# A two-layer diffusion backbone: modulation rows of the second layer made during the first layer's attention instead of beside its experts

## The chip, the core and the metric

The kernel runs on one core of a Trainium2 chip. The core has TensorE (PE in the profile), VectorE (DVE), ScalarE (ACT), GpSimd (POOL) and the DMA queues, of which the kernel uses SyncE's (SP) for nearly all loads and POOL's for gathers, scatters and some tables. The metric is the device time of one execution in microseconds (us), the median of several runs.

## What is computed

Two layers over 1024 latent tokens and 256 context tokens of width 1024. Cut to what matters here:

```python
for l in range(DEPTH):                       # 2 layers
    mod   = silu_c  @ w_ada[l] + b_ada[l]    # 6 x 1024 numbers for the latent tokens
    mod_c = silu_cc @ w_ada[l] + b_ada[l]    # the same for the context tokens
    sh1, sc1, g1, sh2, sc2, g2 = split(mod, 6)
    h = modulate(rms_norm(x, norm1_g[l]), sh1, sc1)
    y, yc = mixer_sublayer(h, hc, ...)       # Fourier | global attention | windowed attention + sink, gated merge
    x = x + g1 * y
    h = modulate(rms_norm(x, norm2_g[l]), sh2, sc2)
    x = x + g2 * expert_choice_ffn(h, ...)   # 16 experts, each takes 128 latent (and 32 context) tokens
    # the same for the context tokens, in layer 0 alone
return rms_norm(x, final_g)
```

`mod` is one row by a 1024 x 6144 matrix. Layer 1 has no context output, so of its modulation the context row is needed for the first 2048 columns alone (shift and scale of the first norm); columns 2048 to 6143 are needed for the latent row only.

## The kernel before

**Stages.** Each layer runs through: norm and modulation, the input projection, attention, the gated merge in chunks of tokens (two of 512 latent tokens, in layer 0 a third of the 256 context tokens), routing (softmax and top-k), and 16 experts. In layer 0 `moe_both` (L1505) runs latent and context tokens of an expert together. Matrix products are made of three passes over pairs (hi, lo): each weight is loaded as float32, ACT casts the hi part (L238), DVE subtracts to get the lo part (L245), and PE multiplies hi by hi, hi by lo and lo by hi. For the first four weight loads of `moe_both` POOL subtracts instead (L243).

**Modulation rows.** They are cut into blocks of 512 columns, called units: `units1` holds layer 1's twelve, the first four with two rows (n = 2), the other eight with one row (n = 1). A unit doesn't use PE for its 1024-deep sum. It multiplies pieces of `w_ada` (128 x 512) by the activation of c, one number a partition, adds eight of them up, and lets PE sum the 128 partitions: two matmuls by a column of ones, for the hi and the lo part of the sum (L337, L338). `ada` (L311) is a generator; `ada_row` (L376) adds the bias row, which it loads from DRAM (L382), multiplies by a norm gain where there is one (L386, L391), and stores the row in DRAM (L399). In the merge of layer 0 the generator runs with ACT doing the products (L351) and POOL the sums (L356): chunk 0 makes layer 0's remaining rows, chunk 1 makes `units1[:6]`. The last six units run in `moe_both`, two steps of the generator at each of the four column blocks of an expert from the second expert on, with POOL doing product and sum, one piece of 256 KB a step: 48 pieces, whose loads (L327) stand in SP's queue among the experts' weight loads (L232).

**Attention.** `attend` records its operations through `Pin`, so all of them have L797 in the profile and keep the order in which they are written on their engine. SP's operations, and those of `ada_row`, aren't pinned: a scheduler puts them where it finds room. 30 groups of queries in layer 0 give 210 steps, one of 128 keys each. A step makes scores on PE into one of two banks (accT), ACT takes the exponential, and PE multiplies by V three steps later (accO). The softmax's maximum comes from a first pass for a later group, spread over the steps: PE makes scores into one of three banks (accS), DVE reduces each to one column of `m` (`rmax`), `mdiag` folds the columns of `m` (and the sink) into `mrs`, and `mrow` transposes that on PE through the same three banks. Where a bank comes up again, `sbank` first runs the reader that was left for it. `outp` copies a group's result out (ACT), for groups with a sink adds the sink's share (DVE), and issues three DMAs on SP; five steps later `recip` takes the reciprocal on DVE of a row that has been to DRAM and back. POOL loads the Fourier tables and is otherwise idle there.

Of the kernel before, what the change touches and what calls it, by code (L numbers as in the profile page):

```python
# [10 lines left out]
F32 = mybir.dt.float32  # L11
F32R = mybir.dt.float32r
# [4 lines left out]
OP = mybir.AluOpType  # L17
AX = mybir.AxisListType
# [90 lines left out]
def f(ap):  # L109
    return ap.bitcast(F32)  # L110
# [7 lines left out]
def hybrid_kernel(ctx, tc, x, c, ctxt, c_ctx, w_ada, b_ada, norm1_g, w_in, q_norm_g, k_norm_g,  # L118
# [17 lines left out]
    def t512(p, n, dt=F32):  # L136
        return tmp.tile([p, n], dt, name="t512")
# [46 lines left out]
    ident = misc.tile([128, 128], F32, name="ident")  # L184
# [11 lines left out]

    gqk = misc.tile([128, 2, 64], F32, name="gqk")
    sinkb = misc.tile([128, 4], F32, name="sinkb")
    mrs = misc.tile([128, 6, 4], F32R, name="mrs")
    mod1 = misc.tile([128, 2, 8, 2], F32, name="mod1")  # L200
    c2 = misc.tile([128, 8, 2], F32, name="c2")
    e2 = misc.tile([128, 4], F32R, name="e2")
# [9 lines left out]
    class Ring:  # L212
# [3 lines left out]
        def load(self, src, kk, n, pool=0):  # L216

            hi, lo, split = self.begin(src, kk, n, pool)
            for _ in split:
                pass  # L220
            return hi, lo
# [605 lines left out]
    def attend(need_ctx, V, S, G, PE):  # L827
# [53 lines left out]
        def prep(g):  # L881
            lab('prep', g['i'])

            for h in range(4):
                PE.transpose(X[0][0:64, 128 * h:128 * h + 128], g["q"][:, 64 * h:64 * h + 64], ident)
            qs = ring("qs", 512, F32R)
            qm = ring("qm", 512, F32R)
            g["qs"], g["qm"] = qs, qm
            g["m"] = st.tile([128, 4, 3], F32, name="m", bufs=4)
            g["us"] = units(g)  # L890
            g["nu"] = len(g["us"]) // 4

        def prep2(g):
            lab('prep', g['i'])
# [35 lines left out]
        def mdiag(g):  # L930
            lab('mdiag', g['i'])
            m = g["m"]
            for i in range(1, g["nu"]):
                V.tensor_max(m[:, :, 0], m[:, :, 0], m[:, :, i])
            if g["sink"]:
                V.tensor_max(m[:, :, 0], m[:, :, 0], sink8)
            g["mr"] = mrs[:, g["i"] % 6]
            V.tensor_copy(g["mr"], m[:, :, 0])

        def mrow(g):  # L940
            lab('mrow', g['i'])
            b = sbank()
            for h in range(4):
                PE.transpose(b[0:1, 128 * h:128 * h + 128], f(g["mr"])[:, h:h + 1], ident)
            S.copy(g["qm"][64:65], b[0:1])

        def scores(g, t):
# [101 lines left out]
        def front():  # L1049
# [25 lines left out]
            mrow(g0)  # L1075
            yield

        def main(hooks):

            ST.extend(acc("T") for _ in range(2))  # L1080
            OB.extend(acc("O") for _ in range(2))
            for o in RINGS["qm"][1:3]:
                qmfill(o)
            fill = fourier_lat(V, S, G, PE, sbank)
            next(fill)
            bk1 = build_k(1, V, S, G, PE, lambda split: X[0])
            kind1 = max(g["s1"] for g in gs if g["ty"] == 1)
            assert min(g["s0"] for g in gs if g["ty"] == 1) >= 20
            for n in range(len(steps) + 4):
                if n < len(steps):  # L1090
                    scores(*steps[n])
                for x in first[n] + acts[n]:
                    x()
                if 2 <= n <= 8:
                    next(bk1, None)
                if n == 9:
                    qmfill(RINGS["qm"][3])
                if n > 8 and n % 2 == 1:
                    next(fill, None)
                if n == kind1 + 6:  # L1100
                    hooks["stage"](G)
                if n == max(kind1 + 12, len(steps) - 30):
                    for _ in fill:
                        pass
                    ld = hooks["weights"](V, S)
                    next(ld)
                if n >= len(steps) - 22 and n % 2 == 0:
                    next(ld, None)
                if 3 <= n < len(steps) + 3:
                    pv(*steps[n - 3])  # L1110
            for _ in ld:
                pass
            return [x for a in acts[len(steps) + 4:] for x in a]
# [391 lines left out]
    def moe_both(l):  # L1505
# [8 lines left out]
        CXL = regr(b + 6144, 1024).rearrange("p (k n) -> p k n", k=8)  # L1514
        X = [regr(b + 7168 + 2560 * i, 2560).rearrange("p (k n) -> p k n", k=8) for i in range(2)]
        ST = [regr(b + 12288, 2560).rearrange("p (k n) -> p k n", k=8)] * 2
        ada_o = [b + 14848 + 512 * i for i in range(5)]
        fill = ada(units1[6:], 1, ada_o[0:2], ada_o[2:3], ada_o[3:5],
                   Pin(V), Pin(G))
        yb = [reg(b + 17408 + 1024 * i, 1024) for i in range(2)]  # L1520
        yc = [reg(b + 19456 + 512 * i, 512) for i in range(2)]
        ycb = reg(b + 20480, 1024)
# [1 line left out]
        for e in range(NE):  # L1524
# [24 lines left out]
            V.tensor_copy(xg[:, :, 288:320], f(CXL[:, :, cc]))  # L1549
            sT = ST[i2]  # L1550
            for fb in range(4):
                for _ in range(2 if e else 0):
                    next(fill, None)
                fs = slice(256 * fb, 256 * fb + 256)
                un = [w_.load(kview(w[l, e, :, fs]), 8, 256, 2 if e == 0 and 2 * fb + t < 4 else 0)
                      for t, w in enumerate((w_gate_e, w_up_e))]
# [43 lines left out]
                V.scalar_tensor_tensor(ycb[0:32, dd], t[0:32], afc[:, e:e + 1], cg2b[0:32, dd], op0=OP.mult, op1=OP.mult)  # L1600
            scatter_add(xd, yb[i2], idxl[:, e:e + 1])
            scatter_add(xcd, ycb[0:32], idx32[:, e:e + 1])
        for _ in fill:
            pass

    def spill(ci, hh, hl, toff, n):
        SP.dma_start(hTd[ci][0], f(hh[toff // 512][:, :, :n]))
# [21 lines left out]
    for l in range(2):  # L1629
# [66 lines left out]
        cut_main()  # L1696
        fills = [iter(())] * 3
        if l == 0:
            todo = [(0, b, 2) for b in (4, 5, 8, 9, 6, 7, 10, 11)] + units1[:6]
            fills = [ada(u, 2, [O_XS + 1024 * i for i in range(2)], [O_XS + 1024 * i for i in range(2, 4)],  # L1700
                         [O_GB + 512 * i for i in range(4)], act=True)
                     for u in (todo[:8], todo[8:], [])]
# [81 lines left out]
```

## Time and profile before

| what | us |
|---|---|
| runs shown (3) | 4038.36, 4061.48, 4057.38; median 4057.38 |
| the profiled execution, its own time | 4049.72 |
| its span, first to last instruction | 4047.9 |
| PE busy in the span | 3726.5 (92%) |
| DVE, ACT, POOL busy | 2803.0, 2023.6, 646.7 |
| attention of layer 0 after the projection | about 262 to 660 |
| merge of layer 0, chunk 1 | about 960 to 1150 |
| experts of layer 0 | about 1400 to 2325 |

How to read it: the span is cut by place, since each stage has its own limit. A window's row gives its length, then for each engine the busy time in it and in brackets the number of instructions (PE, PE's weight loads, DVE, ACT, POOL), the granted TensorE clock as a share of full speed, the mean busy share of the DMA engines, and GB/s. A row of grouped instructions gives line, engine, operation, tiles (output <- inputs), shapes and count, then busy us and the mean ns of one, then the idle time of the engine just before them and what ended it. A timeline row gives start and length in us, then the instruction, and in brackets the idle time before it and what ended that. A row of waits gives who waited for what: us in total, times, longest.

### The profile page before, as it was taken

How to read it: one execution, taken by the hardware profiler on the slowest of the kernel's cores; microseconds unless marked ns; L12 is line 12 of the kernel's file. 1: busy time of each engine (PE TensorE's matmuls, PEld its weight loads, DVE VectorE, ACT ScalarE, POOL GpSimd, SP SyncE). 2: the span in 40 equal slices, each digit the busy share in tenths (PEclk: the TensorE clock that was granted, in tenths of full speed). 3: DMA queues.
4: the chain of work that ended last, by engine and by line, in shares of the span. 5: the costliest groups of instructions: out<-in, count | busy, mean ns of one | idle time of the engine just before them, and what ended most of it. 6: DMA issues, size and time to landing. Idle time of an engine off the chain costs nothing.

```text
span 4047.9 us, 52394 instructions
## 1 busy us (share of the span) xinstructions
PE 3726.5 (92%) x19185; PEld 2952.5 (73%) x19185; DVE 2803.0 (69%) x5007; ACT 2023.6 (50%) x3181; POOL 646.7 (16%) x598
## 2 busy tenths in 40 slices
PE   7989998899999698999999979999999994999997
PEld 4766655688789687788888867666588884777775
DVE  5855556957658677888777667455445746899988
ACT  4235555534424365556666542555433331777775
POOL 0230003512400423342000013100000002011100
PEclk9999999999999799999999989999999996999999
DMA  7332013555556477777877550401235435999996
GB/s 249 128 57 65 12 53 105 179 170 186 188 174 204 164 251 255 235 258 253 263 251 246 189 192 19 96 14 52 74 99 177 148 118 177 351 376 376 380 376 243
DMA packets 491503, 749.07 MB, mean 185 GB/s; under 512 B 27216, under 2 KB 291664, under 8 KB 489962
## 3 DMA queue, kind: packets, MB, share of 16 engines
q1 hardware_dynamic: 453996, 654.14, 46.9%
q0 software_dynamic: 32064, 72.70, 7.2%
q10 hardware_dynamic: 5184, 18.88, 1.2%
q8 instruction: 151, 2.47, 0.3%
q14 instruction: 108, 0.88, 0.1%
HBM read 675.21 MB, written 70.52 MB: 184 GB/s over the span
## 4 chain that ended last, share of the span: by engine, by line
PE 58%; DVE 15%; issue 14%; DMA 7%; ACT 4%; POOL 2%; SPq 0%; POOLq 0%; DVEq 0%; ACTq 0%
PE accA L259 10%; PE accA L261 10%; PE accA L260 10%; PE accO L797 8%; PE accT L797 5%; DVE a_r L245 4%; PE accS L797 4%; PE accA L1566 2%; PE accA L1564 2%; DMA a_f<-in_w_in_dram 2%; DMA a_f<-in_w_ada_dram 1%; ACT a_r L238 1%; DMA a_f<-in_w_down_e_dram 1%; DVE a_f L358 1%; POOL a_f L797 1%
## 5 line engine op out<-in xcount | busy, mean ns | idle before, releaser
L245 DVE TENSOR_TENSOR a_r<-a_f,a_r 128x1024 fp32r<-128x1024 f32 (+1 forms) x1008 | 1220.2, 1230 | 370.3 <-ACT a_r L238 346.1
L238 ACT CAST a_r<-a_f 128x1024 fp32r<-128x1024 f32 (+1 forms) x1024 | 1030.6, 1029 | 700.2 <-DVE a_r L245 281.5
L259 PE MATMUL accA<-a_r,a_r 128*128 128x512 f32 (+1 forms) x2816 | 1039.7, 370 | 33.3 <-DVE a_f L1596 8.7
L261 PE MATMUL accA<-a_r,a_r 128*128 128x512 f32 (+1 forms) x2816 | 1028.4, 367 | 21.7 <-DVE a_r L245 15.3
L260 PE MATMUL accA<-a_r,a_r 128*128 128x512 f32 (+1 forms) x2816 | 1032.3, 367 | 10.5 <-DVE a_f L1169 6.2
L259 PEld LDWEIGHTS accA<-a_r,a_r 128*128 128x128 f32 x2816 | 539.6, 192 | 152.5 <-DVE a_f L1596 11.5
L261 PEld LDWEIGHTS accA<-a_r,a_r 128*128 128x128 f32 x2816 | 538.8, 192 | 116.2 <-DVE a_r L245 19.8
L260 PEld LDWEIGHTS accA<-a_r,a_r 128*128 128x128 f32 x2816 | 539.8, 192 | 96.9 <-DVE a_r L245 8.5
L1566 PE MATMUL accA<-a_r,a_r 128*128 128x320 f32 x2048 | 537.9, 314 | 16.3 <-DVE a_f L1574 15.4
L1564 PE MATMUL accA<-a_r,a_r 128*128 128x256 f32 x1792 | 485.1, 283 | 0.0
L797 DVE TENSOR_REDUCE m<-accS 128x1 f32<-128x512 f32 (+2 forms) x536 | 284.8, 559 | 199.4 <-PE accS L797 195.5
L797 PE MATMUL accO<-a_f,a_f 128*65 128x512 f32 (+1 forms) x976 | 418.6, 525 | 0.0
L797 ACT ACTIVATE a_f<-accT 128x512 f32<-128x512 f32 x408 | 243.4, 597 | 312.7 <-PE accT L797 308.7
L1566 PEld LDWEIGHTS accA<-a_r,a_r 128*128 128x128 f32 x2048 | 373.6, 190 | 20.4 <-DVE a_f L1574 17.5
L1564 PEld LDWEIGHTS accA<-a_r,a_r 128*128 128x128 f32 x1792 | 345.7, 193 | 0.6
L797 PE MATMUL accT<-a_r 128*128 128x512 f32 x512 | 257.2, 583 | 1.6 <-ACT a_f L797 1.6
L259 PE MATMUL accO<-a_r,a_r 128*128 128x512 f32 (+1 forms) x464 | 186.8, 405 | 19.2 <-ACT a_f L561 11.5
L797 PEld LDWEIGHTS accT<-a_r 128*128 128x128 f32 x512 | 97.4, 191 | 125.7 <-issue 107.5
L260 PE MATMUL accO<-a_r,a_r 128*128 128x512 f32 (+1 forms) x464 | 182.7, 396 | 2.8 <-DVE a_r L245 2.6
L261 PE MATMUL accO<-a_r,a_r 128*128 128x512 f32 (+1 forms) x464 | 181.5, 394 | 0.2 <-DVE a_r L472 0.2
L797 PEld LDWEIGHTS accO<-a_f,a_f 128*65 128x65 f32 x976 | 128.7, 138 | 44.5 <-issue 3.3
L356 POOL TENSOR_TENSOR a_f<-a_f,a_f 128x512 f32<-128x512 f32 x84 | 141.5, 1685 | 88.3 <-ACT a_f L351 78.1
(288 smaller groups left out, 4722.6 us busy)
## 6 DMA issues: line engine op xcount, KB each, us to landing
a_f<-in_w_gate_e_dram SPq DMA_DIRECT2D x128, 1024.0 KB
a_f<-in_w_up_e_dram SPq DMA_DIRECT2D x128, 1024.0 KB
a_f<-in_w_down_e_dram SPq DMA_DIRECT2D x128, 1024.0 KB
a_f<-in_w_in_dram SPq DMA_DIRECT2D x60, 1024.0 KB
a_f<-in_w_ada_dram SPq DMA_DIRECT2D x60, 512.0 KB
a_f<-in_w_out_dram SPq DMA_DIRECT2D x20, 1024.0 KB
a_f<-in_w_in_dram SPq DMA_DIRECT2D x36, 512.0 KB
hTd<-a_r SPq DMA_DIRECT2D x8, 2048.0 KB
```

The lines of the kernel that those rows point to most:

```text
L238: S.copy(hi[:, c], raw[:, c])
L245: V.tensor_sub(lo[:, c], raw[:, c], f(hi[:, c]))
L259: PE.matmul(ps, lhsT=lh, rhs=rh, start=start, stop=False)
L260: PE.matmul(ps, lhsT=lh, rhs=rl, start=False, stop=False)
L261: PE.matmul(ps, lhsT=ll, rhs=rh, start=False, stop=stop)
L356: G.tensor_tensor(acc_[0], prod[:, 0] if h == 0 else acc_[0], prod[:, k], op=OP.add)
L358: V.scalar_tensor_tensor(acc_[1], w[:, k], c2[:, kk * h + k, 1:2], zero.to_broadcast([128, 512]) if h + k == 0 else acc_[1], op0=OP.mult, ...
L797: return lambda *a, **k: tc.keep_in_program_order(fn(*a, **k))
L1564: PE.matmul(ps[:, 512 * t:512 * t + 256], lhsT=wl[:, k, fc], rhs=xg[:, k, 0:256], start=False, stop=False)
L1566: PE.matmul(ps[:, 512 * t:512 * t + 320], lhsT=wh[:, k, fc], rhs=xg[:, k, 0:320], start=k == 0, stop=k == 7)
```

## The change

1. `units1[4:]`, all eight units with one row, are made in the main part of layer 0's attention by two new functions. `rows1` does the products and sums on POOL, one piece of 256 KB a call, called at steps 12, 15, 17, 20, 22 and so on (two in five) into two raw buffers and two sums; the cast and the subtraction that split a finished sum go to ACT and DVE three pieces later. `sums_out` then takes one of the three accS banks for the two matmuls, and leaves `ada_row` as that bank's reader.
2. The generator in `moe_both` is gone, and chunk 1 of the merge makes `units1[:4]` instead of `units1[:6]`.
3. `mdiag` makes the maximum in one TENSOR_REDUCE over the columns of `m`; the sink's values are copied into a column of `m` in `prep`. `mrs` becomes plain float32.

```diff
-    mrs = misc.tile([128, 6, 4], F32R, name="mrs")
+    mrs = misc.tile([128, 6, 4], F32, name="mrs")
...
             g["nu"] = len(g["us"]) // 4
+            if g["sink"]:
+                V.tensor_copy(g["m"][:, :, g["nu"]], sink8)
...
             m = g["m"]
-            for i in range(1, g["nu"]):
-                V.tensor_max(m[:, :, 0], m[:, :, 0], m[:, :, i])
-            if g["sink"]:
-                V.tensor_max(m[:, :, 0], m[:, :, 0], sink8)
             g["mr"] = mrs[:, g["i"] % 6]
-            V.tensor_copy(g["mr"], m[:, :, 0])
+            V.tensor_reduce(g["mr"], m[:, :, 0:g["nu"] + g["sink"]], axis=AX.X, op=OP.max)
...
+        def rows1(units, raws, prod, accs):
+            pieces = [(l, b, h) for l, b, _ in units for h in range(8)]
+            def load(i):
+                if i < len(pieces):
+                    l, b, h = pieces[i]
+                    SP.dma_start(reg(raws[i % 2], 512), w_ada[l, 128 * h:128 * h + 128, 512 * b:512 * b + 512])
...
+            for i, (l, b, h) in enumerate(pieces):
+                a = reg(accs[i // 8 % 2], 512)
+                p = reg(prod, 512) if h else a
+                G.tensor_tensor(p, reg(raws[i % 2], 512), c2[:, h, 0:1].to_broadcast([128, 512]), op=OP.mult)
+                load(i + 2)
+                if h:
+                    G.tensor_tensor(a, a, p, op=OP.add)
+                yield
+                if h == 2 and todo:
+                    todo()
+                if h == 7:
+                    def todo(l=l, b=b, a=a):
+                        hi, lo = t512(128, 512, F32R), t512(128, 512, F32R)
+                        S.copy(hi, a)
+                        V.tensor_sub(lo, a, f(hi))
+                        sums.append((l, b, hi, lo))
...
+        def sums_out(l, b, hi, lo):
+            ps = sbank(lambda: ada_row(l, b, ps[0:1], t512(1, 512), n=1))
+            PE.matmul(ps[0:1], lhsT=e2[:, 0:1], rhs=hi, start=True, stop=False)
+            PE.matmul(ps[0:1], lhsT=e2[:, 0:1], rhs=lo, start=False, stop=True)
...
+                if n == 12:
+                    ada1 = rows1(units1[4:] if need_ctx else [], [10752, 11264], 11776, [O_K, O_K + 512])
+                if n >= 12:
+                    if sums and n % 2 == 0:
+                        sums_out(*sums.pop(0))
+                    if n % 5 in (0, 2):
+                        next(ada1, None)
...
-        fill = ada(units1[6:], 1, ada_o[0:2], ada_o[2:3], ada_o[3:5],
-                   Pin(V), Pin(G))
...
-                for _ in range(2 if e else 0):
-                    next(fill, None)
...
-            todo = [(0, b, 2) for b in (4, 5, 8, 9, 6, 7, 10, 11)] + units1[:6]
+            todo = [(0, b, 2) for b in (4, 5, 8, 9, 6, 7, 10, 11)] + units1[:4]
```

How instructions move, at three places. On **POOL**, at the start of layer 0's experts (`hd,idxl` and `hcd,idxc` are the gathers of an expert's latent and context tokens, the second waited for by the first expert; `xd` and `xcd` are its scatters; 128x256 is a weight's lo part, 128x512 the generator's products and sums). Before:

```order
L243 TENSOR_TENSOR a_2048_r<-a_2048_f,a_2048_r 128x256 x2
L797 TENSOR_TENSOR a_512_f<-a_512_f,c_95 128x512
L243 TENSOR_TENSOR a_2048_r<-a_2048_f,a_2048_r 128x256
L797 TENSOR_TENSOR a_512_f<-a_512_f 128x512
L243 TENSOR_TENSOR a_2048_r<-a_2048_f,a_2048_r 128x256
L797 TENSOR_TENSOR a_512_f<-a_512_f,c_95 128x512
L797 TENSOR_TENSOR a_512_f<-a_512_f 128x512
L797 DMA a_1024_f<-hcd,idxc 128x1024
L1406 DMA a_1024_f<-hd,idxl 128x1024
L1410 DMA xd<-a_1024_f,idxl 1024x1024
L1410 DMA xcd<-a_1024_f,idx_131 256x1024
L797 TENSOR_TENSOR a_512_f<-a_512_f,c_95 128x512 x2
```

And now (L1456 and L1460 are the old L1406 and L1410):

```order
L243 TENSOR_TENSOR a_2048_r<-a_2048_f,a_2048_r 128x256 x14
L1456 DMA a_1024_f<-hd,idxl 128x1024
L243 TENSOR_TENSOR a_2048_r<-a_2048_f,a_2048_r 128x256 x6
L797 DMA a_1024_f<-hcd,idxc 128x1024
L1456 DMA a_1024_f<-hd,idxl 128x1024
L1460 DMA xd<-a_1024_f,idxl 1024x1024
L1460 DMA xcd<-a_1024_f,idx_131 256x1024
L1456 DMA a_1024_f<-hd,idxl 128x1024
```

The products and sums are gone from between the lo parts, from before the context gather, and from between scatters and gathers.

On **SP**, in the attention (`sdd`, `od`, `rd` and `rdd` are the DMAs of `outp` and `recip`, of which `rd` waits until `sdd` has landed). Before:

```order
L997 DMA sdd<-a_512_f 1x512
L998 DMA od<-a_512_f 64x4x128
L1000 DMA rd<-sdd 16x32
L998 DMA odc<-a_512_f 64x4x128
L997 DMA sdd<-a_512_f 1x512
L1000 DMA rd<-sdd 16x32
L1006 DMA rdd<-rd 16x32 x2
```

And now (L995 to L1004 are the old L997 to L1006; L1084 is a load of `rows1`, L382 the bias row, L399 the finished row):

```order
L382 DMA t_3446<-in_b_ada_dram 1x512
L998 DMA rd<-sdd 16x32
L1084 DMA a_512_f<-in_w_ada_dram 128x512 x2
L399 DMA modd_71<-t_3445 1x512
L1084 DMA a_512_f<-in_w_ada_dram 128x512
L1004 DMA rdd<-rd 16x32
L1084 DMA a_512_f<-in_w_ada_dram 128x512 x5
L995 DMA sdd<-a_512_f 1x512
L996 DMA od<-a_512_f 64x4x128
L998 DMA rd<-sdd 16x32
```

Eight loads of a unit now stand close together ahead of a group's output, and the bias row stands ahead of them.

On **DVE**, in the attention near step 40 (each `m<-accS` is a row maximum from a bank). Before:

```order
L797 TENSOR_REDUCE m<-accS 128x1 x4
L797 TENSOR_TENSOR m<-m 128x4
L797 TENSOR_TENSOR m<-m,sink_400 128x4
L797 CAST mrs<-m 128x4
L797 TENSOR_REDUCE m<-accS 128x1 x2
```

And now:

```order
L797 TENSOR_TENSOR t_3130<-a_512_f,t_3129 128x512
L797 TENSOR_REDUCE m<-accS 128x1 x4
L797 TENSOR_REDUCE mrs<-m 128x4
L797 TENSOR_REDUCE m<-accS 128x1
L389 TENSOR_TENSOR t_3185<-accS,t_3186 1x512
L797 TENSOR_REDUCE m<-accS 128x1
```

Three small operations are one; the subtraction of a unit's sum and the bias addition stand in the line with the row maxima.

## Rows read from the trace of the kernel before

**Rows 1.** Windows: layer 0's attention, expert 0, experts 1-8, experts 9-15.
```profile
262.00:660.00 398.00, 381.96 (x1678) 236.92 (x1677) 203.65 (x442) 220.31 (x408) 24.53 (x42) 0.99 0.19 47
...
1400.00:1457.00 57.00, 57.00 (x359) 51.37 (x359) 40.66 (x68) 35.00 (x61) 0.98 (x2) 0.97 0.64 213
1457.00:1942.00 485.00, 451.39 (x2780) 394.18 (x2779) 389.44 (x547) 280.88 (x491) 167.37 (x102) 0.96 0.77 251
1942.00:2321.00 379.00, 374.80 (x2394) 332.71 (x2392) 286.28 (x454) 232.65 (x416) 27.02 (x19) 1.00 0.73 239
```
**Rows 2.** Timeline, POOL: the scatters that end the first, ninth and last expert.
```profile
1456.95 1.62 POOL L1410 DMA_INDIRECT xd<-a_f,idxl  x1 [54.71 <-DVE a_f L1596]
...
1941.93 1.58 POOL L1410 DMA_INDIRECT xd<-a_f,idxl  x1 [53.39 <-DVE a_f L1596]
...
2321.43 1.55 POOL L1410 DMA_INDIRECT xd<-a_f,idxl  x1 [49.50 <-DVE a_f L1596]
```
**Rows 3.** Grouped instructions, DVE, 1500 to 1900: experts with the generator.
```profile
L245 DVE TENSOR_TENSOR a_r<-a_f,a_r 128x1024 fp32r<-128x1024 f32 x153 | 206.3, 1360 | 56.7 <-ACT a_r L238 56.3
L1574 DVE TENSOR_TENSOR a_f<-accA,a_f 128x320 f32<-128x320 f32 x50 | 24.2, 484 | 13.5 <-ACT a_f L1573 13.1
L1577 DVE TENSOR_TENSOR t<-t,a_f 128x160 f32<-128x160 f32 x50 | 23.2, 464 | 4.4 <-ACT t L1576 4.4
```
**Rows 4.** Grouped instructions, DVE, 1900 to 2310: experts without it.
```profile
L245 DVE TENSOR_TENSOR a_r<-a_f,a_r 128x1024 fp32r<-128x1024 f32 x178 | 215.4, 1220 | 67.2 <-ACT a_r L238 67.0
L1574 DVE TENSOR_TENSOR a_f<-accA,a_f 128x320 f32<-128x320 f32 x62 | 30.2, 486 | 10.7 <-ACT a_f L1573 9.9
L1577 DVE TENSOR_TENSOR t<-t,a_f 128x160 f32<-128x160 f32 x62 | 19.8, 320 | 6.5 <-ACT t L1576 6.5
```
**Rows 5.** Waits of SP's queue, 1376 to 1900.
```profile
SPq L327 <- POOL a_f L797: 87.9, 32, 7.8
```
**Rows 6.** Timeline, ACT, 1524 to 1537: a weight that came late.
```profile
1534.56 1.04 ACT L238 CAST a_r<-a_f 128x1024 fp32r<-128x1024 f32 x1 [8.97 <-DMA a_f<-in_w_up_e_dram]
```
**Rows 7.** Timeline, POOL, before the first expert.
```profile
1389.57 1.03 POOL L797 TENSOR_TENSOR a_f<-a_f,c 128x512 f32<-128x512 f32 x1
...
1392.09 0.96 POOL L797 DMA_INDIRECT a_f<-hcd,idxc  x1
```
**Rows 8.** Timeline, DVE, before the first expert: the context gather's indices.
```profile
1386.63 0.64 DVE L797 CAST idxc<-accT 32x4 int32<-32x4 f32 x4
```
**Rows 9.** Timeline, PE, before the first expert: what waits for that gather.
```profile
1396.57 1.94 PE L1543 MATMUL accT<-ident,a_f 128*128 128x128 f32 x8 [10.16 <-DMA a_f<-hcd,idxc]
```
**Rows 10.** Timeline, SP, 1060 to 1102: chunk 1 of the merge.
```profile
1068.10 10.55 SPq L327 DMA_DIRECT2D a_f<-in_w_ada_dram  x3
```
**Rows 11.** One line, L337: a unit's matmul.
```profile
L337 PE MATMUL accC<-t,e x32: 387/392/585, 694.0 to 1899.0; 128*2 128x512 f32 x24, 128*1 128x512 f32 x8
```
**Rows 12.** One line, L382: who waited for bias rows.
```profile
  DVE t L389: 8.9, 3
```
**Rows 13.** Waits of PE, 262 to 660: attention of layer 0.
```profile
PE accS L797 <- DVE m L797: 5.7, 7, 2.3
PE accS L797 <- DVE mrs L797: 3.3, 4, 1.5
```
**Rows 14.** Grouped instructions, DVE, 262 to 660: the folding of the maxima.
```profile
L797 DVE TENSOR_TENSOR m<-m 128x4 f32<-128x4 f32 x38 | 5.9, 155 | 0.7
```
**Rows 15.** Waits of DVE, 262 to 660.
```profile
DVE rd L797 <- DMA rd<-sdd: 10.9, 3, 5.9
```
**Rows 16.** Timeline, DVE, 1360 to 1367: the same operation twice.
```profile
1361.05 4.58 DVE L285 SCALAR_TENSOR_TENSOR rsq<-rsy,ss 128x1 f32<-128x1 f32 x1
...
1365.86 0.22 DVE L285 SCALAR_TENSOR_TENSOR rsq<-rsy,ss 128x1 f32<-128x1 f32 x1
```
**Rows 17.** Timeline, POOL, 1359 to 1367: beside that operation.
```profile
1360.28 3.43 POOL L243 TENSOR_TENSOR a_r<-a_f,a_r 128x256 fp32r<-128x256 f32 x5
1363.68 1.25 POOL L797 TENSOR_TENSOR a_f<-a_f 128x512 f32<-128x512 f32 x1
```

More of the change, by code (lines that the diff above doesn't have):

```diff
@@ L943, in mrow @@
             for h in range(4):
-                PE.transpose(b[0:1, 128 * h:128 * h + 128], f(g["mr"])[:, h:h + 1], ident)
+                PE.transpose(b[0:1, 128 * h:128 * h + 128], g["mr"][:, h:h + 1], ident)
             S.copy(g["qm"][64:65], b[0:1])
@@ L1076, in front @@
             yield
+        def rows1(units, raws, prod, accs):
[4 more added lines that the diff above has]
+                    SP.dma_start(reg(raws[i % 2], 512), w_ada[l, 128 * h:128 * h + 128, 512 * b:512 * b + 512])
+            todo = None
+            if not pieces:
+                return
+            load(0)
+            load(1)
+            for i, (l, b, h) in enumerate(pieces):
[14 more added lines that the diff above has]
+                        sums.append((l, b, hi, lo))
+            yield
+            todo()
+            yield
+        def sums_out(l, b, hi, lo):
+            ps = sbank(lambda: ada_row(l, b, ps[0:1], t512(1, 512), n=1))
+            PE.matmul(ps[0:1], lhsT=e2[:, 0:1], rhs=hi, start=True, stop=False)
+            PE.matmul(ps[0:1], lhsT=e2[:, 0:1], rhs=lo, start=False, stop=True)
+        sums = []
         def main(hooks):
@@ L1104, in main @@
                         pass
+                    for _ in ada1:
+                        pass
+                    while sums:
+                        sums_out(*sums.pop(0))
                     ld = hooks["weights"](V, S)
@@ L1516, in moe_both @@
         ST = [regr(b + 12288, 2560).rearrange("p (k n) -> p k n", k=8)] * 2
-        ada_o = [b + 14848 + 512 * i for i in range(5)]
-        fill = ada(units1[6:], 1, ada_o[0:2], ada_o[2:3], ada_o[3:5],
-                   Pin(V), Pin(G))
         yb = [reg(b + 17408 + 1024 * i, 1024) for i in range(2)]
@@ L1602, in moe_both @@
             scatter_add(xcd, ycb[0:32], idx32[:, e:e + 1])
-        for _ in fill:
-            pass
     def spill(ci, hh, hl, toff, n):
```

## The prediction, made before the change was run

> **What bounds the kernel now.** I read the windows first, then the scatters that end an expert, then DVE's operations and the waits of the two stretches that the change joins: the experts of layer 0, from which work goes, and its attention, into which work comes. The reader is to see three things.
>
> First, the experts run at two speeds. A scatter ends each expert: experts 1 to 8 lie between the scatters at 1456.95 and 1941.93, so 484.98/8 = 60.6 us each; experts 9 to 15 between 1941.93 and 2321.43, so 379.50/7 = 54.2 us each [rows 2]. The difference is what the generator runs beside: POOL is busy 167.4 of 485 us in the slow stretch and 27.0 of 379 in the quick one. PE is busy 451.4 of 485 in the one and 374.8 of 379 in the other, and its granted clock has a mean of 0.96 against 1.00, so part of the slow stretch passed at the lower of its two levels (1.2 rather than 2.4 GHz). The first expert, which has no step of the generator, keeps PE busy for all of its 57 us [rows 1].
>
> Second, how the generator does it. DVE's lo part takes 1360 ns on average beside it and 1220 without, the product L1577, both of whose operands are in SBUF, 464 against 320; L1574, which reads PSUM, takes 484 and 486 [rows 3, 4]. And SP's queue waited 87.9 us in 32 places for POOL before it could issue a generator's load, up to 7.8 us [rows 5], with weight loads behind it: one up weight kept ACT waiting for 8.97 us [rows 6], and PE with it.
>
> Third, the attention of layer 0 has POOL nearly free (24.5 of 398 us) and the DMA engines 19% busy, but PE is busy 382.0 of 398 [rows 1]. What is added there on PE or in PE's waits counts; what is added on POOL, SP and the DMA engines counts only by what it delays.
>
> **The parts of the change.** The sum is made against the profiled execution, 4049.7 us; the median of the runs shown, 4057.4, lies 7.7 above it.
>
> *Experts.* All 48 steps go from experts 1 to 8. I take the rate of the seven experts behind them: 484.98 - 8 x 54.2 = 51.4 us saved. This includes the twelve matmuls, the casts and the bias rows that go too. The DMA share is 0.77 and 0.73 [rows 1], so the weights alone did not fill the DMA engines in either stretch.
>
> *Before the first expert.* The context gather's indices are ready at 1386.63 + 0.64 = 1387.3, and POOL starts the gather at 1392.1, behind a product, a sum and lo parts; PE waits for it until 1396.6 [rows 7 to 9]. Without the generator POOL should be through its lo parts: 4.8 us. At most the operation of DVE that took 4.58 instead of 0.22 us a little earlier [rows 16] is helped as well: 9.2.
>
> *Merge, chunk 1.* It loses two of its six units: eight loads, sixteen products on ACT, fourteen sums on POOL, four matmuls. The view of SP shows 10.6 us in which three such loads held the queue [rows 10]; PE was seldom waiting there for anything of these two units. Between 0 and 10.6 I take 2.
>
> *Matmuls in the attention.* Sixteen at 0.39 us [rows 11] on a PE that is full: 6.3 us. They pass in the shadow of nothing.
>
> *Waits in the attention.* POOL's 64 products and 56 sums take 1.03 and 1.25 us when nothing disturbs them [rows 7, 17], about 18 us a unit of eight pieces. A step of the attention takes 398/214 = 1.9 us, so the 20 steps from unit to unit last 37 us: POOL keeps up, and a unit's sum is ready long before ACT comes to cast it. The 16.8 MB are some 55 GB/s over 165 steps, beside 47 GB/s [rows 1]. On DVE come eight subtractions, eight bias additions and two gains: 1 to 3 us a unit, on an engine that is half idle (203.7 of 398). A bias addition waits for its row from DRAM; where that showed before, it took 8.9 us in three places [rows 12], 3.0 us each. Behind it stand row maxima, for whose banks PE waits. Eight times 3.0 are 24 us at most; the order puts the row's load ahead of the unit's next loads, which are what SP waits with, so I take 4.
>
> *DVE beside POOL.* New in the attention is that DVE works beside a busy POOL. The row maxima read PSUM, like L1574, which was not slowed. About 28 operations have operands in SBUF alone: eight subtractions, ten copies of the sink, ten additions of the sink's share. At the 0.14 us by which L1577 grew that is 4 us of DVE, half of it seen: 2. The far end is the 4.4 us by which one operation grew [rows 16], while POOL passed six operations without a gap [rows 17]: 28 times that, 123 us.
> The Trainium skill's page "SBUF — State Buffer" (section "SBUF: two separate sides") has the rule behind this: VectorE and GpSimd share a port pair, an operation of VectorE with two SBUF inputs, or in a mode that uses both ports, excludes one of GpSimd that reads SBUF, and the loser waits for the whole instruction. That speaks against this change. By it an affected operation would wait for the rest of one product or sum, half of 1.1 us on average, 16 us of DVE in all instead of 4, and the sum would be 6 us worse. The two operations above agree with the rule as to who is slowed; the 4.58 us, longer than any one instruction of POOL beside it, do not agree with it as to how long.
>
> *Maxima in one operation.* Three dependent small operations (155 ns for one of the first two [rows 14]) become one in all 54 groups of both layers. DVE doesn't bound the attention; PE waited 3.3 us in four places for the folded maximum in layer 0 [rows 13]. Both layers together: 2 us saved, between 0 and 3.3 for layer 0 alone.
>
> Sum: -51.4 - 4.8 - 2 + 6.3 + 4 + 2 - 2 = -47.9 us. From the profiled execution that gives 4001.8, from the median 4009.5; I give the middle, **4006 us**.
>
> **Rivals.**
> *The attention gives it back in part.* The reciprocals stand on DVE in front of row maxima, and wait for a row that SP must send out and fetch. They waited before, 10.9 us in three places [rows 15], and now SP's queue also holds loads that wait for POOL: 2.75 us each in the experts [rows 5]. 24 reciprocals fall among the loads; if each comes 2.75 us late and half of that reaches PE, that is 33 us: about 4039. For it: loads and outputs share one queue, eight loads at a time. Against: a reciprocal has five steps, 9 us, for its two transfers.
>
> *The attention loses more than the experts gain.* One mechanism: DVE's SBUF operations starve beside POOL as one did there [rows 16, 17]. At 4.4 us for each of 28, all of it reaching PE, the time is 4006 - 2 + 123 = 4127. It decides from about 2.4 us an operation on (the 48 saved and the 20 that a measurement must see, over 28). Against: in the experts' stretch, where POOL was busy a third of the time, the same kind of operation grew by 0.14 us on average, and POOL pauses here between pieces, for their loads.
>
> *The experts don't gain.* If what slows experts 1 to 8 were the filling of the weight buffers after routing, the generator was beside it by chance, and only the gather and the merge gain: 4050. For it: it is the early experts that are slow. Against: expert 0 and the start of expert 1, before POOL's products begin, have PE full; POOL's stretches and PE's gaps fall together.
>
> **How the numbers follow.** About 0.5%, 20 us, is what a measurement of this kernel can tell from no change. My forecast gets 0.74, the first rival 0.13, the second 0.05, the third 0.08. The forecast's own range: at best 51.4 + 9.2 + 10.6 + 3.3 - 6.3 = 68 saved, 3982 from the profiled execution; at worst the bias rows cost 24 rather than 4, and DVE beside POOL 8 rather than 2: about 4032. Taking in half of the first rival the range is 3980 to 4040. Faster by over 0.5% (below 4037): all of the forecast and a third of the first rival, 0.79; within 0.5%: most of the rest of that and the third rival, 0.15; slower: 0.06.
>
> **What would show it.** Right: all experts of layer 0 at 54 us from scatter to scatter, lo parts at 1220 ns throughout, no wait of SP for POOL there; the context gather issued within 1 us of its indices; in the attention sixteen more matmuls, PE still at 96%, and the stretch from its first to its last step not over 15 us longer. Wrong: PE waits on `m`, `mrs` or bias additions of tens of us in the attention (the first rival if reciprocals wait for `rd`, the second if small DVE operations take several us), or early experts that stay at 60 us.

## The result, and the profile after

The changed kernel takes 3995.95 us (median of 4 runs, 3991.48 to 4000.33), the kernel before 4051.98 (4 runs, one more than shown above, 4038.36 to 4061.48). The ratio is 0.9875, 95% interval 0.9857 to 0.9894: 51 us less, between 43 and 58. The profiled execution took 3996.45 us, its span is 3994.7 against 4047.9.

Windows of the changed kernel, in the places of [rows 1]: attention of layer 0 (the window is 15 us longer), experts 1 to 8, experts 9 to 15.

```profile
262.00:675.00 413.00, 390.04 (x1692) 238.99 (x1692) 213.42 (x422) 224.51 (x415) 163.29 (x161) 0.98 0.31 86
1454.00:1891.00 437.00, 432.86 (x2772) 384.95 (x2772) 339.62 (x534) 276.25 (x485) 35.38 (x27) 1.00 0.78 255
1891.00:2269.00 378.00, 374.49 (x2392) 332.48 (x2390) 286.64 (x454) 232.57 (x416) 27.02 (x19) 1.00 0.74 240
```

Timeline of POOL, the scatters of [rows 2]: experts 1 to 8 now take (1890.96 - 1454.29)/8 = 54.6 us, experts 9 to 15 54.1.

```profile
1454.29 1.62 POOL L1460 DMA_INDIRECT xd<-a_f,idxl  x1 [54.40 <-DVE a_f L1641]
...
1890.96 1.58 POOL L1460 DMA_INDIRECT xd<-a_f,idxl  x1 [53.06 <-DVE a_f L1641]
...
2269.42 1.55 POOL L1460 DMA_INDIRECT xd<-a_f,idxl  x1 [49.48 <-DVE a_f L1641]
```

Grouped instructions of DVE, 1450 to 1850, the lines of [rows 3] under their new numbers: they stand where [rows 4] stood.

```profile
L245 DVE TENSOR_TENSOR a_r<-a_f,a_r 128x1024 fp32r<-128x1024 f32 x175 | 211.8, 1221 | 65.2 <-ACT a_r L238 65.0
L1619 DVE TENSOR_TENSOR a_f<-accA,a_f 128x320 f32<-128x320 f32 x59 | 28.8, 488 | 13.0 <-ACT a_f L1618 12.1
L1622 DVE TENSOR_TENSOR t<-t,a_f 128x160 f32<-128x160 f32 x58 | 18.6, 320 | 6.0 <-ACT t L1621 6.0
```

Before the first expert, timelines of DVE, POOL and PE in this order: the context gather starts 0.3 us behind its indices (1389.48), against 4.8 in [rows 7, 8].

```profile
1388.84 0.64 DVE L797 CAST idxc<-accT 32x4 int32<-32x4 f32 x4
...
1389.75 0.95 POOL L797 DMA_INDIRECT a_f<-hcd,idxc  x1 [0.71 <-DVE idxc L797]
...
1394.22 1.94 PE L1590 MATMUL accT<-ident,a_f 128*128 128x128 f32 x8 [5.59 <-DMA a_f<-hcd,idxc]
```

Where the time went, stage by stage. The attention's last matmuls of PE show how it is worked out; first before, then after:

```profile
655.48 3.60 PE L797 MATMUL accO<-a_f,a_f 128*65 128x512 f32 x8
```

```profile
671.51 3.60 PE L797 MATMUL accO<-a_f,a_f 128*65 128x512 f32 x8
```

They come 16.0 us later; its first came 0.5 later, so it is 15.5 us longer. The table does that at seven marks. Its other rows are the runs of the next section, each one execution against the same one of before.

| us against before | attention 262–655 | merge chunk 0 to 1000 | chunk 1 to 1154 | third part to 1340 | routing to 1398 | experts 0–8 to 1942 |
|---|---|---|---|---|---|---|
| the change | +15.5 | +2.4 | -7.3 | -4.5 | -8.9 | -48.9 |
| the change, once more | +13.3 | +5.0 | -7.4 | -3.1 | -9.0 | -48.8 |
| maxima alone | -1.5 | +1.2 | -1.5 | -1.4 | -0.5 | +2.5 |
| without the maxima | +18.4 | +5.2 | -5.9 | -3.8 | -9.8 | -49.4 |
| six units moved | +11.2 | +2.6 | -4.8 | -2.8 | -9.9 | -46.8 |
| before, arithmetic, no loads | +0.2 | +1.6 | 0.0 | -2.6 | +0.8 | -10.9 |
| before, products, no loads | -0.7 | +2.6 | -0.9 | -3.6 | -2.5 | -30.6 |
| before, loads, hardly arithmetic | +0.2 | +0.7 | -1.5 | -1.8 | -7.8 | -40.3 |
| loads on POOL's queue | +8.1 | +2.8 | -7.8 | -2.5 | -8.7 | -48.2 |
| subtraction later (two runs) | +11.2, +5.9 | +2.7, +3.9 | -5.6, -4.5 | -6.0, -1.3 | -9.2, -8.9 | -48.3, -48.6 |
| both of these (two runs) | +7.1, +7.0 | +3.8, +4.8 | -5.2, -6.0 | -1.3, -6.2 | -9.1, -9.8 | -48.6, -45.4 |

Where a run leaves a stage as it was, its entry shows how far that stage moves by itself: mostly up to 3 us. In the third part, which no run alters, the entries lie between -1.3 and -6.2; all are shorter, so the one execution of before was long there. Two executions of the same kernel differ by up to 5.3 us in a stage: in the attention with the subtraction later, +11.2 and +5.9, the granted clock from 262 to 672 is 0.98 in the first and 1.00 in the second. A difference of under 5 us between two single entries therefore decides nothing alone.

### The profile page after: what moved, and what is told of

Same layout as the page of the kernel before. It is cut to its first block, busy times and chain, and to the rows that moved or that the text cites. A ratio compares the mean times of both kernels' runs of the same rounds, so it can differ in the third digit from the quotient of the medians.

```text
span 3994.7 us, 52289 instructions
## 1 busy us (share of the span) xinstructions
PE 3712.4 (93%) x19185; PEld 2941.9 (74%) x19185; DVE 2749.0 (69%) x4927; ACT 2013.0 (50%) x3165; POOL 616.6 (15%) x614
## 4 chain that ended last, share of the span: by engine, by line
PE 49%; issue 24%; DVE 13%; DMA 7%; ACT 3%; POOL 3%; SPq 0%; POOLq 0%; DVEq 0%; ACTq 0%
PE accA L261 10%; PE accA L259 10%; PE accA L260 10%; PE accO L797 7%; PE accT L797 4%; DVE a_r L245 3%; PE accS L797 3%; POOL a_f L797 2%; DMA a_f<-in_w_ada_dram 1%; DVE a_f L358 1%; DMA a_f<-in_w_in_dram 1%; PE accO L260 1%; DMA xd<-a_f,idxl 1%; PE accO L259 1%; PE accO L261 1%
## 5 line engine op out<-in xcount | busy, mean ns | idle before, releaser
L245 DVE TENSOR_TENSOR a_r<-a_f,a_r 128x1024 fp32r<-128x1024 f32 (+1 forms) x1008 | 1196.7, 1207 | 366.2 <-ACT a_r L238 342.7
L797 PE MATMUL accO<-a_f,a_f 128*65 128x512 f32 (+1 forms) x976 | 419.6, 526 | 0.0
L797 DVE TENSOR_REDUCE m<-accS 128x1 f32<-128x512 f32 (+2 forms) x536 | 284.3, 558 | 193.6 <-PE accS L797 190.4
L797 ACT ACTIVATE a_f<-accT 128x512 f32<-128x512 f32 x408 | 243.4, 597 | 323.0 <-PE accT L797 317.2
L797 PE MATMUL accT<-a_r 128*128 128x512 f32 x512 | 258.4, 586 | 1.6 <-ACT a_f L797 1.6
L797 PEld LDWEIGHTS accT<-a_r 128*128 128x128 f32 x512 | 97.9, 192 | 126.4 <-issue 107.9
L797 PEld LDWEIGHTS accO<-a_f,a_f 128*65 128x65 f32 x976 | 128.9, 138 | 45.6 <-issue 4.2
L1274 ACT ACTIVATE a_f<-accA 128x512 f32<-128x512 f32 (+1 forms) x120 | 66.2, 552 | 176.0 <-PE accA L261 175.0
```

The source lines that it names most:

```text
L245: V.tensor_sub(lo[:, c], raw[:, c], f(hi[:, c]))
L797: return lambda *a, **k: tc.keep_in_program_order(fn(*a, **k))
L1274: S.activation(sg, gp, AF.Sigmoid)
```

## The experiments

**What in the generator cost the experts their time: three runs of the kernel before.** The first leaves out all but two of its loads:

```diff
-            if i < len(pieces):
+            if i < len(pieces) and (kk > 1 or i < 2):
                 l, b, _, h = pieces[i]
```

> The kernel before, whose generator in the experts keeps all its products, sums, splits and matmuls but loads only its first two pieces (12.1 MB of 12.6 MB of loads left out; the later products read those two pieces again, so layer 1's gate row and second modulation are not the reference's). Theory queue (SP's queue stands while a load waits for POOL, weight loads behind it): experts 1 to 8 fall from 60.6 to 54 to 56 us, the time to about 4005 to 4015, although POOL stays 167 us busy and L1577 stays near 464 ns. Theory port (VectorE slowed beside POOL's arithmetic): experts 1 to 8 stay at 59 to 61 us, the time within 10 us of before. Theory traffic (the extra bytes): as queue in time, and then the next run decides.

4040.75 us (median of 8 runs; ratio 0.9978, 0.9967 to 0.9989). The second keeps the loads and leaves out most of the arithmetic:

```diff
-            else:
+            elif kk > 1 or h == 0:
                 G.tensor_tensor(prod, w, c2[...
...
-                if h + k:
+                if h + k and kk > 1:
                     G.tensor_tensor(acc_[0], ...
```

> The kernel before, whose generator in the experts keeps all its 48 loads but makes only the first product of each unit and no sum (42 of 48 products and all 42 sums left out; the rows are not the reference's), so that no load waits for POOL any more. Theories queue and port: experts 1 to 8 at 54 to 55 us, the time about 4003 to 4010. Theory traffic: they stay at 59 to 61 us, the time within 10 us of before.

4004.72 us (2 runs; 0.9893, 0.9869 to 0.9916). The third takes the first edit and the sums' half of the second.

> As the run with the arithmetic alone, but the 42 sums are left out too: of POOL's arithmetic in the experts the 48 products are left (about 50 of 112 us; the rows are not the reference's). Theory port (an operation of VectorE with SBUF operands waits for the POOL operation beside it): the cost goes with POOL's busy time, so that of the 4.3 us an expert by which 59.3 lies above 55.0 (the later experts' 54.2 and the generator's own matmuls and bias rows) about 45% stays: 57 us an expert, the time about 4022; L1577 near 375 ns. Rival (it is not the busy time but that any operation of the generator stands in POOL's queue in front of a gather or scatter): the 48 places are the same, 58.5 to 59.5 us an expert, 4035 or more.

4016.64 us (4 runs; 0.9909, 0.9887 to 0.9931). Window of the old experts 1 to 8 (1457 to 1942), the product L1577, and the scatters that begin and end them; first with all arithmetic and no loads:

```profile
1457.00:1942.00 485.00, 458.65 (x2861) 401.22 (x2861) 396.55 (x559) 286.77 (x504) 180.72 (x103) 0.99 0.74 237
L1577 DVE TENSOR_TENSOR t<-t,a_f 128x160 f32<-128x160 f32 x66 | 29.4, 445 | 6.5 <-ACT t L1576 6.5
1456.63 1.62 POOL L1410 DMA_INDIRECT xd<-a_f,idxl  x1 [54.66 <-DVE a_f L1596]
...
1930.73 1.57 POOL L1410 DMA_INDIRECT xd<-a_f,idxl  x1 [54.91 <-DVE a_f L1596]
```

With the products alone and no loads:

```profile
1457.00:1942.00 485.00, 469.67 (x2993) 417.02 (x2993) 386.45 (x588) 301.96 (x531) 112.36 (x66) 0.99 0.76 246
L1577 DVE TENSOR_TENSOR t<-t,a_f 128x160 f32<-128x160 f32 x70 | 24.8, 354 | 6.5 <-ACT t L1576 6.5
1451.67 1.62 POOL L1410 DMA_INDIRECT xd<-a_f,idxl  x1 [53.73 <-DVE a_f L1596]
...
1907.02 1.57 POOL L1410 DMA_INDIRECT xd<-a_f,idxl  x1 [53.39 <-DVE a_f L1596]
```

With all loads and hardly any arithmetic:

```profile
1457.00:1942.00 485.00, 478.46 (x3024) 421.51 (x3023) 379.27 (x598) 306.91 (x536) 47.30 (x33) 1.00 0.81 263
L1577 DVE TENSOR_TENSOR t<-t,a_f 128x160 f32<-128x160 f32 x70 | 22.3, 319 | 6.4 <-ACT t L1576 6.4
1445.92 1.63 POOL L1410 DMA_INDIRECT xd<-a_f,idxl  x1 [54.68 <-DVE a_f L1596]
...
1890.61 1.57 POOL L1410 DMA_INDIRECT xd<-a_f,idxl  x1 [53.39 <-DVE a_f L1596]
```

That is 59.3, 56.9 and 55.6 us an expert, against 60.6 before and 54.6 now. Without the loads 10.9 us are gained, without the arithmetic 40.3 (with it go most of SP's waits: 14.7 us of the 87.9 are left, where none were expected), by the change 48.9. So the arithmetic is worth between 29 (40.3 - 10.9) and 38 (48.9 - 10.9, where matmuls, casts and bias rows of the generator are included), and queue and traffic fall as the main cause. Less arithmetic costs less: with the products alone about half of POOL's added busy time is left (112.4 against 180.7, with 47.3 where hardly any is made), and a third to a half of the cost (9.7 of 29.4, or 18.3 of 38.0); 57 us an expert was expected, and the rival's 58.5 falls. PE waits for no gather in any of these windows; in the first, its longest entries are for DVE:

```profile
PE accA L1566 <- DVE a_f L1574: 8.3, 9, 2.2
PE accA L259 <- DVE a_f L1596: 6.1, 3, 2.9
```

Without the arithmetic these two are 0.5 and 1.2 us. All of PE's waits in the window add up to 26 us in the first run and 6 in the second: 20 of the 29 us. The rest passes with PE busy, 56.1 us an expert against 54.9, at a mean granted clock of 0.99 against 1.00. What the loads cost shows in the kernel before, where the first of the two entries has one wait of 9.9 us, behind the late weight of [rows 6]:

```profile
PE accA L1566 <- DVE a_f L1574: 15.4, 7, 9.9
```

How a wait for DVE beside POOL comes about, from the first run's timelines (POOL, three of DVE, PE): a product of POOL holds up L1581; L1574, which reads PSUM and takes its usual 0.48 us, starts late behind it, and PE waits.

```profile
1520.51 1.90 POOL L797 TENSOR_TENSOR a_f<-a_f,c 128x512 f32<-128x512 f32 x1
...
1521.43 1.12 DVE L1581 TENSOR_TENSOR a_r<-t,a_r 128x128 fp32r<-128x128 f32 x1
1522.48 0.18 DVE L1582 TENSOR_TENSOR a_r<-t,a_r 128x32 fp32r<-128x32 f32 x1
1522.59 0.48 DVE L1574 TENSOR_TENSOR a_f<-accA,a_f 128x320 f32<-128x320 f32 x1
...
1523.12 0.41 PE L1566 MATMUL accA<-a_r,a_r 128*128 128x320 f32 x1 [0.73 <-DVE a_f L1574]
```

**The two parts of the change apart.** The change without its maxima:

```diff
-            V.tensor_reduce(g["mr"], m[:, :, 0:g["nu"] + g["sink"]], axis=AX.X, op=OP.max)
+            for i in range(1, g["nu"]):
+                V.tensor_max(m[:, :, 0], m[:, :, 0], m[:, :, i])
...
```

> The change without its part on the maxima (folded by two to three small operations as before). If the maxima are worth 2 us, as forecast, the time is about 3998 and PE waits for the folded maximum in layer 0's attention about as before, 3.3 us in four places instead of 1.8 in two. If they are worth more, because the shorter chain keeps the attention from running into its new waits, the attention of layer 0 is over 5 us longer than with the whole change.

4004.94 us (4 runs; 0.9887, 0.9867 to 0.9906); the attention is 18.4 us longer than before, 3 to 5 more than with the maxima; the expectation set over 5 as its mark. PE's waits for the folded maximum:

```profile
PE accS L797 <- DVE mrs L797: 5.9, 4, 2.6
```

And the maxima alone, on the kernel before:

> The kernel before with the maxima in one operation, and nothing else of the change. Forecast: 2 us (0 to 5) off the time, 4047 to 4051; PE's waits for the folded maximum in layer 0's attention, 3.3 us in four places, fall under 2. The rest of the program is before's, so the trace also shows how far a stage that nothing changed in (the merges, the routing) moves from one execution to the next: by 1 us if the 7 and 14 us that the change won there are its own, by 5 us or more if they are not.

4048.06 us (10 runs; 0.9994, 0.9982 to 1.0005): no difference that can be measured. In the attention it is 1.5 us, and the same waits are 1.7 us in two places:

```profile
PE accS L797 <- DVE mrs L797: 1.7, 2, 1.1
```

By these waits the maxima are worth 1.6 us alone (3.3 to 1.7) and 4.1 beside the generator (5.9 to 1.8). That they are worth more beside a busy POOL rests on the waits alone: neither the times nor the attention's entries, one or two executions each, can show 3 us.

**Chunk 1 of the merge.** With `units1[4:6]` back in chunk 1 (`rows1(units1[6:] ...)` and `+ units1[:6]`):

> The change with units1[4:6] left in chunk 1 of the merge, as before; the six units of the experts alone are made in the attention. If the 7 us that chunk 1 got shorter come from its two units, they come back, and the attention is 3 to 4 us shorter than with the whole change (two units of eight at 2 us each): about 3999 to 4001, experts unchanged at 54.6 us. If chunk 1 got shorter for another reason (its place in time, the loads of the experts behind it), it keeps the 7 us and the time is 3990 to 3993.

4000.79 us (4 runs; 0.9884, 0.986 to 0.9909). The attention is 2 to 4 us shorter than with the change, where 3 to 4 were expected. Chunk 1 is 4.8 us shorter than before with its two units in place. In the eight executions without them it is 4.5 to 7.8 shorter, so what the two units cost there can't be told from nothing; it is 2.5 us against the first execution of the change. What most of the 4.8 is from stays open; by the runs that left chunk 1 alone, up to 1.5 of it can be chance.

**The attention.** Loads on POOL's queue:

```diff
-                    SP.dma_start(reg(raws[i % 2], 512), w_ada[l, ...
+                    G.dma_start(reg(raws[i % 2], 512), w_ada[l, ...
```

> The change with the 64 loads of its attention part issued on POOL's queue instead of SP's; PE, DVE and ACT have the same instructions in the same order. Theory of the shared queue (four loads that waited for POOL held SP's queue for 8 us, a group's sum went out late, a reciprocal waited 5.2 us on DVE and PE 3.9 us, and then 5 us at the lower clock): the wait of the reciprocal falls under 2 us, that stall of PE is gone, and layer 0's attention is 6 to 8 us shorter than with the change; the time about 3988 to 3990. Rival, issuing costs POOL too much: 64 issues at 0.6 us (what its other loads take) leave POOL behind the steps, DVE's operations stand longer beside it, and the attention is as long or longer; 3996 or more.

3995.93 us (4 runs; 0.9867, 0.985 to 0.9885). The attention is 5 to 7 us shorter, the reciprocal in question no longer waits, and the stall of PE behind it, 3.87 us in the change, is 0.75, as the theory of the shared queue had it; the time forecast from that, 3988 to 3990, did not come. The subtraction one call later:

```diff
                         S.copy(hi, a)
+                        yield
                         V.tensor_sub(lo, a, f(hi))
```

> The change with the subtraction of a unit's split one call (two to three steps) behind ACT's cast instead of right behind it. If DVE's waits for that cast (16.7 us in eight places) hold back row maxima that PE needs, they fall under 3 us, PE's waits for row maxima fall from 8.2 to 6 us, and the attention is 2 to 3 us shorter: 3993 to 3994. Rival: DVE has time for it, PE's waits were for something else; no difference in the attention, 3996.

3991.43 us (4 runs; 0.9861, 0.984 to 0.9882). DVE's waits for that cast are gone, PE's for row maxima are 6.6 us, and the attention is 2 to 4 us shorter than with the change, all near what was expected. Both together:

> Both edits on top of the change: the loads on POOL's queue, and the subtraction one call later. If the two stalls are independent of each other, the attention is 8 to 11 us shorter than with the change and the time 3985 to 3988; if POOL's queue is too slow for the loads, 3994 or more.

3998.71 us (4 runs; 0.9864, 0.9846 to 0.9883), although the attention is 6 to 8 us shorter than with the change. To see whether that was chance, the change and the two versions once more side by side:

> The change itself, unaltered, beside the next two: about 3996. How far its attention and its other stages move from its first execution to this one is the bound for what the next two can show.

> Loads on POOL's queue and the subtraction one call later, once more. If the 8.7 us that its attention gained are kept and the 10 us that it lost behind the attention were chance of that execution (PE, DVE and ACT have the same order there), the time is 3985 to 3990, 6 to 10 us under the change in the same call. If it loses them again, they belong to the edit: 3995 or more.

> The subtraction one call later alone, once more: the attention 4 to 5 us shorter than the change's and the time 3990 to 3993, if the first execution was typical; within 2 us of the change if not.

The change: 4000.93 (5 runs; 0.9872, 0.9852 to 0.9892). Both edits: 3994.28 (5 runs; 0.9847, 0.9828 to 0.9867). The subtraction alone: 3996.14 (5 runs; 0.9861, 0.9841 to 0.9881). The intervals overlap: no version can be told from the change by its time, and neither expectation was met: 3994.28 lies between the two values set for both edits, 3996.14 above the 3990 to 3993 for the subtraction. What the traces do show is the stall at one place in the attention: 3.1 to 3.9 us in all six executions that load on SP's queue during it, the two of the change and the two of the subtraction alone among them, and 0.75, 2.1 and 2.1 in the three that load on POOL's. The attention's length shows it less well: +7.0 to +8.1 with POOL's queue, +15.5 and +13.3 with the change, but +11.2 and +5.9 with the subtraction alone. And stages that no version alters move as much: the change's second execution ends 6.1 us later than its first, of which 4.2 arose behind the experts of layer 0.

Part of why POOL's queue gained no time stands at the end of the program, where POOL issues the last scatter. It starts at 3989.94 in the change, 4.7 us before the end of its span, and at 3984.75 with the loads on POOL's queue, 8.3 us before the end. First the change, then that version:

```profile
3989.94 0.97 POOL L1551 DMA_INDIRECT out_dram<-a_f,idxl  x1 [43.04 <-DMA out_dram<-a_f]
```

```profile
3984.75 0.98 POOL L1551 DMA_INDIRECT out_dram<-a_f,idxl  x1 [44.25 <-DMA out_dram<-a_f]
```

Both executions with both edits end 8.3 and 8.4 us behind that scatter as well; in the eleven other kept traces it is 4.7 to 5.1. Why the kernel ends later there was not tried.

## Why the prediction was right, step by step

The forecast was 4006 us, the middle of two values that a sum of -47.9 gave. The profiled execution lost 53, the medians differ by 56, and the ratio says 43 to 58. The direction, the place and the size hold, but the sum is right partly by luck, because terms that were off cancel: the experts gave 2.5 less and the attention cost 5.2 more than forecast, the stretch before the first expert gave 4.1 and chunk 1 5.3 more. Another 4.5 came in the third part, which the change doesn't touch. Of the signs, all came that concern the experts; in the attention PE is busy 94% of its window rather than 96, and the 15.5 and 13.3 us that it is longer lie on both sides of the 15 that was set.

*Experts, -51.4: right, -48.9 with expert 0.* The rate of the later experts was the right price for the whole. The explanation gave equal weight to two mechanisms, and here the runs decide: SP's 87.9 us of waits were worth 11 at most, POOL's arithmetic about three times as much. The third rival, that the early experts are slow for another reason, falls with the run of the loads alone. Its time, 4050, was mispriced too: it left out the 10 us that the sum adds in the attention, and would have been 4006 + 51 = 4057.

*Before the first expert, -4.8: too small, -8.9.* The gather gave about what was forecast: its indices come 2.2 us later than before and PE's matmul behind it starts 2.35 us earlier, 4.6 in all. The rest came in front of it, and the arithmetic is what does it: without it the routing is 7.8 us shorter, with it and without loads 0.8 longer. The far end, 9.2, was near the number, but by luck: its reason, the 4.58 us operation of [rows 16], is not needed for the loss. With the maxima alone, where POOL's arithmetic stays, that operation takes 0.67 us (timeline of DVE) and the routing is only 0.5 us shorter.

```profile
1358.51 0.67 DVE L285 SCALAR_TENSOR_TENSOR rsq<-rsy,ss 128x1 f32<-128x1 f32 x1
```

*Chunk 1, -2: -7.3 came.* What the term named, the two units, is 2.5 by one pair of executions and can't be told from nothing; most of the rest came with the units in place, was not foreseen and is not explained.

*Matmuls, +6.3: too large.* The step took the duration of a matmul. In a full PE the next begins before the last has ended; timeline of PE in the changed kernel:

```profile
371.37 0.62 PE L797 MATMUL accS<-t,e 128*1 128x512 f32 x2
371.83 1.02 PE L797 MATMUL accO<-a_f,a_f 128*65 128x256 f32 x4
```

Two take 0.46 us from start to start, eight pairs 3.7 us.

*Waits in the attention, +4 for bias rows: the place was wrong, and it was more.* PE's waits from 262 to 675:

```profile
PE accS L797 <- DVE m L797: 8.2, 10, 2.5
PE accS L797 <- DVE a_r L797: 5.7, 3, 3.9
...
PE accS L797 <- DVE mrs L797: 1.8, 2, 1.2
...
PE accS L797 <- DVE t L389: 0.5, 1, 0.5
```

Before, the first was 5.7, the third 3.3 [rows 13], and the second was

```profile
PE accS L797 <- DVE a_r L797: 0.9, 1, 0.9
```

Bias additions (L389) cost 0.5, in the second execution of the change 1.9; row maxima cost 2.5 more than before, and `a_r` 4.8. The 3.9 in it is the first rival's mechanism, once. Timelines of SP, DVE and PE around it:

```profile
450.59 7.74 SPq L1084 DMA_DIRECT2D a_f<-in_w_ada_dram  x4
458.42 0.24 SPq L995 DMA_DIRECT2D sdd<-a_f  x1
...
460.91 0.38 SPq L998 DMA_DIRECT2D rd<-sdd  x1
...
463.40 0.34 DVE L797 RECIPROCAL rd<-rd 16x32 f32<-16x32 f32 x1 [5.18 <-DMA rd<-sdd]
...
466.02 0.69 PE L797 MATMUL accS<-a_r,a_r 128*128 128x384 f32 x1 [3.87 <-DVE a_r L797]
...
466.74 1.92 PE L797 MATMUL accO<-a_f,a_f 128*65 128x512 f32 x2
```

Four loads that wait for POOL hold SP's queue for 7.7 us, a sum goes out behind them, DVE waits for its way back, PE for DVE. Then PE runs at the lower level of its clock (0.50 granted, 1.2 GHz) until about 471, a pair of matmuls taking 1.92 us instead of 1.02:

```profile
466.00:471.00 5.00, 4.98 (x16) 2.77 (x17) 1.53 (x4) 1.17 (x2) 0.00 (x0) 0.50 0.01 3
```

The wait cost 3.9 us and the matmuls behind it 2.8 more (5.8 us, where the same ones took 3.05 before). The lower clock did not follow each time: of the six executions with such a wait, four show it and two, behind waits of 3.7 and 3.2 us, do not. The rival priced 24 of these at half of 2.75 us; it was one of 6.7. The other wait that the prediction lacks is DVE's for ACT's cast of a sum, 16.7 us in eight places (`DVE t L797 <- ACT t L797`). With the subtraction moved it goes, and PE's waits for row maxima fall by 1.6 us.

*DVE beside POOL, +2: twice as much on DVE, from the copies.* Against the durations that undisturbed ones of the same kind have in this trace (0.17, 0.69, 0.68 us), the ten copies of the sink take 4.9 us more, the eight subtractions 1.1, the ten additions of the sink's share 1.5: 7.5 us of DVE, where 4 were forecast. The subtractions and additions lost 0.14 us each, the very price of the prediction; the copies, short operations of which eight met POOL's arithmetic, 0.49 each. With the maxima alone, where POOL makes no products or sums beside them, no copy takes over 0.17. What of the 7.5 reached PE was not measured. Groups of DVE in the attention:

```profile
L797 DVE TENSOR_TENSOR a_f<-a_f 1x512 f32<-1x512 f32 x10 | 8.3, 832 | 13.6 <-ACT a_f L797 13.5
L797 DVE TENSOR_TENSOR t<-a_f,t 128x512 fp32r<-128x512 f32 x8 | 6.6, 826 | 16.7 <-ACT t L797 16.7
L797 DVE COPY m<-sink 128x4 f32<-128x4 f32 x10 | 6.6, 658 | 0.1
```

The second rival priced each at 4.4; none took over 1.8. And the prediction set a rule of the Trainium skill (page "SBUF — State Buffer", section "SBUF: two separate sides": whichever of the two engines starts first holds the shared ports for its whole instruction, and the other stands) below a mean of 0.14 us. One by one, the trace agrees with the rule. Timelines of POOL and DVE:

```profile
294.95 1.06 POOL L797 TENSOR_TENSOR a_f<-a_f,c 128x512 f32<-128x512 f32 x1
...
295.03 1.02 DVE L797 COPY m<-sink 128x4 f32<-128x4 f32 x1
...
376.38 0.68 DVE L797 TENSOR_TENSOR a_f<-a_f 1x512 f32<-1x512 f32 x1 [0.23 <-ACT a_f L797]
...
376.60 1.60 POOL L797 TENSOR_TENSOR a_f<-a_f 128x512 f32<-128x512 f32 x1
```

POOL first: the copy ends 0.04 us behind POOL's product. DVE first: DVE takes its usual 0.68 us and POOL's sum 1.60 instead of 1.28. The mean of 0.14 in [rows 3] hides this: 41 of the 50 took 0.31 to 0.33 us, nine 0.82 to 1.64. The estimate made by the rule, 16 us, lacked the share of the time in which POOL is busy, 163 of 413 us; with it the estimate is 6, near the 7.5.

*Maxima, -2: right as far as can be seen*, 1.6 us of PE's waits alone and 4.1 beside the generator.

The attention in all: forecast +10, measured +15.5 and +13.3. Of the 15.5, matmuls (3.7), PE's longer waits for row maxima, `a_r` and the generator's own rows (8.1), the lower clock behind the stall (2.8) and the maxima (-1.5) explain 13; the rest was not found. Merge chunk 0, to which the prediction gave nothing, is 2 to 5 us longer in every version with the move and 1 to 3 in those without; that is too small to be told from chance.

## What to carry to other kernels

Work that is put on POOL as free is paid for by operations of DVE on SBUF beside it: put it where DVE mostly reads PSUM, and price it by the share of time in which POOL runs, times what is left of one of its instructions. That estimate is rough: 6 us for the 28 operations here against 7.5 measured, and 0.2 us for an operation like L1577 in the experts against 0.14. Count short operations as well, since they lost as much each as long ones or more. A load that must wait for a slow engine does not belong in a queue behind which short loops of other engines (here: a sum out, its reciprocal in) wait for their data; here it cost up to 6.7 us at one place, though moving the loads won no time that could be measured. Two mechanisms that a profile shows side by side, here 88 us of queue waits and 0.1 us a DVE operation, are told apart by leaving one out; here the one with the larger row was the smaller cost.

## What the runs showed of the hardware that was not expected

- Not all operations of DVE with SBUF operands are slowed beside POOL. A RECIPROCAL of 16x32 took 0.33 to 0.34 us at all 13 places in the attention where POOL's arithmetic ran beside it, and the new reduction over `m` 0.17 us at most at 11 such places, as without; a copy of 128x4 took 0.5 to 1.0 instead of 0.17 at eight of ten.
- The 4.58 us of [rows 16] stayed alone: in the changed kernel no operation of DVE took over 1.2 us more than the shortest of its kind, about one instruction of POOL. In the thirteen other traces that same operation took 1.57 us at most. Why that one waited for six was not tried.
- With 64 loads issued on POOL's queue the program ended 3.6 us later behind its last scatter, over 3300 us after the last of those loads, in all three such executions.
- A stall of PE of 3.1 to 3.9 us at the same place was followed by the lower clock in four executions and not in two.
